# Ordering the loads of the state-space batches behind the load of the in-chunk kernel

## The chip, the cores and the metric

The kernel runs on one core of a Trainium2 chip. The metric is the device time of one launch in microseconds (us); before the change the median of three runs is 1145.79 us (1145.49 to 1152.16). A core has engines that each work through their own queue in order: PE (TensorE, matrix products), DVE (VectorE), ACT (ScalarE), POOL (GpSimd) and SP (SyncE, which here issues most of the transfers). An instruction whose inputs aren't there holds up all that stands behind it on its engine, and that goes for a transfer on SP's queue too.

## The reference, cut to what matters

The reference is a two-layer streaming encoder over 1024 frames of width 1024. Layer 0 has a state-space branch beside a retention branch, each multiplied by a SiLU gate; layer 1 is a convolution module. The change touches the state-space branch alone. For each of 64 groups of 16 channels it runs a diagonal complex recurrence with 64 states:

```
bu = einsum('tbgh,gnh->tbgn', u_c, bb)      # inputs into the states, bb complex
x  = scan: x[t] = a * x[t-1] + bu[t]        # a complex, diagonal
y  = einsum('tbgn,ghn->tbgh', x, c) + d * u_c   # real part
```

## The kernel before, in words

The kernel takes the frames in 128 blocks of 8. Inside a block the result is a product of u with an in-chunk kernel; between the blocks the states are carried by a scan. The 64 groups are worked off in eight batches of 8 groups, B = 0 to 7. The loop in `layer0_front` runs over sixteen gate blocks (nb = 8 to 23, two for each batch). A gate block has two halves of 24 matmuls (`mm_g`, each 128x512). Around them, in the order of the program text, stand for batch B:

- `s5_states(B)`: the load of u for the batch (tile `U`, L850); the matmuls `v` (L868), which put u through the two matrices `W2r` and `W2i`; on DVE the turning of `v`, the two scans over the blocks (L883) and the shifted states `S` (L890 to L896); the matmuls `kp` (L902, L903), which give the in-chunk kernel; its copies `Kg` (L905 on ACT, L906 on DVE), its transpose `kt` on PE (L908), its copy `Kt` on ACT (L910); the store of `Kt` to DRAM (L912); and the load of the same kernel in shifted form, tile `Wd` (L915), which ACT copies into `W1` (L917).
- the first gate block.
- `s5_out(B-1)`: the matmuls `y` of the batch before, u times `W1` (L932) and `S` times `W3` (L938), and their copies `yb`.
- the second gate block.
- `s5_tables(B+1)`: on POOL eighteen products for the tables of the next batch (`Mr`, `Mi`, `Tc`, `Ts`, `W3`); on ACT four copies that make `R8` (L839), the factors of the next scan; and for B+1 of 2 and more `s5_w2(B+1)`, which loads the spread tables `PTr`, `PTi`, `BTr` and `BTi` (L799 and L802, 256 KB each) and makes `W2r` and `W2i` out of them in six DVE instructions (L806 to L811). For batches 0 and 1 `W2` comes from transposes on PE instead.

Most of these tiles have one buffer: `PT`, `BT`, `W2`, `R8`, `S`, `W1`, `Mr`, `Mi`. `U` has two. `Wd` and the copies `yb` share a single buffer. The weights of the gate blocks come in by `wf_g` (L187 on SP), are rounded by ACT (`wh_g`, L189), and DVE forms the remainder (`wl_g`, L190). The gate results leave PSUM through DVE (`gt`, L393) and ACT (L394).

The order on each engine is fixed at build time by a list scheduler, which takes the ready instruction that stands first in the program text. `tc.issue_after(x)` adds a rule of order to it: what the block traces on the engine of x is put behind x in that engine's queue. It is an order of issue alone and waits for nothing to finish. Before the change one such rule exists here: the spread tables of batch B+1 are queued behind `self.u_load`, which at that point is the load of `U` for batch B.

Of the kernel before, what the change touches and what calls it, by code (L numbers as in the profile page):

```python
# [19 lines left out]
P = 128  # L20
# [50 lines left out]
class Trunk:  # L71
# [22 lines left out]
    def plan(self):  # L94

        A = self.A

        seq = [(A["w_u01"][nb] if nb < 2 else A["w_ab"][nb], f"u{nb}") for nb in range(8)]
        seq += [(A["w_ab"][nb], f"g{nb}") for nb in range(8, 24)]
        for p in range(4):  # L100
            seq += [(A["w_ab"][28 + p], f"k{p}"), (A["w_ab"][24 + p], f"q{p}")]

            if p == 0:
                seq += [(A["w_v"][j], f"v{p}_{h}_{j}") for h in range(2) for j in range(4)]
            elif p > 1:
                seq += [(A["w_v"][2 * p + i], f"v{p}_{i}") for i in range(2)]
        self.ws_d = self.dram.tile([2, 2, P, 2, KB, P], F32, name="ws_d")
        quad = lambda i, j, m: A["w_glu"][i, m, :, j]
        sums = lambda n, m: self.ws_d[n // 2, m, :, n % 2]
        glu = [q for m in range(2) for q in (quad(0, 0, m), quad(0, 1, m))]  # L110
        glu += [q(m) for q in (lambda m: sums(0, m), lambda m: sums(2, m), lambda m: quad(1, 1, m)) for m in range(2)]
        glu += [sums(n, m) for m in range(2) for n in (3, 1)]
        seq += [(q, f"glu{i}") for i, q in enumerate(glu)]

        def wo(h):
            return [q for nb in range(8) for q in ((A["w_out"][nb], f"wos{nb}_{h}"),
                                                   (A["w_out"][8 + nb], f"wor{nb}_{h}"))]

        def ab(h):
            return [q for nb in range(8) for q in ((A["w_c"][8 + nb], f"cb{nb}_{h}"),  # L120
                                                   (A["w_c"][nb], f"ca{nb}_{h}"))]
        def cg(h, nbs):
            return [(A["w_c"][16 + nb], f"cg{nb}_{h}") for nb in nbs]
        seq += wo(0) + wo(1)[:4] + ab(0) + wo(1)[4:] + cg(0, range(G0)) + ab(1) + cg(0, range(G0, 8))
        seq += cg(1, range(G0))
        seq += [(A["w_out_c"][nb], f"woc{nb}_{h}") for h in range(2) for nb in range(8)]
        self.wseq, self.wissued, self.wgot = seq, {}, 0
        self.low_load, self.early_low = {}, None
        self.wnames, self.lo_d = {n for _, n in seq}, {}

    def wnext(self, name, ahead=2):
# [659 lines left out]
    def s5_w2(self, B):  # L791

        nc, v = self.nc, self.nc.vector
        (ptr, pti), (btr, bti) = ([self.big(f"{n}{c}_{B}", f"{n}{c}", 1) for c in "ri"] for n in ("PT", "BT"))
        dp, db = self.pt_d, self.bt_d

        with self.tc.issue_after(self.u_load.ins):
            for c, (pt, bt) in enumerate(((ptr, btr), (pti, bti))):
                nc.sync.dma_start(pt[:].rearrange("p q n -> p (q n)"),  # L799
                                  bass.AP(tensor=dp.tensor, offset=dp.offset + (c * 2 * P + 4 * B) * P,  # L800
                                          ap=[[32 * P, 8], [0, 16], [1, 4 * P]]))
                nc.sync.dma_start(bt[:].rearrange("p q n -> p (q n)"),  # L802
                                  bass.AP(tensor=db.tensor, offset=db.offset + (c * 4 * P + 4 * B) * P,
                                          ap=[[0, 8], [32 * P, 16], [1, 4 * P]]))
        w2r, w2i = (self.big(f"W2{nm}_{B}", f"W2{nm}", 1) for nm in "ri")
        v.tensor_tensor(w2r[:], ptr[:], btr[:], op=ALU.mult)  # L806
        v.tensor_tensor(w2i[:], ptr[:], bti[:], op=ALU.mult)
        v.tensor_tensor(ptr[:], pti[:], bti[:], op=ALU.mult)
        v.tensor_tensor(pti[:], pti[:], btr[:], op=ALU.mult)
        v.tensor_tensor(w2r[:], w2r[:], ptr[:], op=ALU.subtract)  # L810
        v.tensor_tensor(w2i[:], w2i[:], pti[:], op=ALU.add)  # L811
        return [w2r, w2i]
# [29 lines left out]
    def s5_states(self, B):  # L842
        nc, w = self.nc, self.s5
        gp, v = nc.gpsimd, nc.vector
        q0 = 4 * B
        Mr, Mi, W3, Tc, Ts, R8, W2 = self.s5_tab.pop(B)


        U = w.tile([P, 8, P], F32, name=f"U_{B}", tag="U", bufs=2)
        self.u_load = nc.sync.dma_start(U[:], self.u_d[B].rearrange("j h g m -> (j h) g m"))  # L850


        first, W2 = W2 is None, W2 or []
        for nm, M in (("r", Mr), ("i", Mi)) if first else ():
            ps = self.bank(f"w2{nm}_{B}")
            for q in range(4):
                nc.tensor.transpose(ps[:, q * P:(q + 1) * P], M[:, q, :], self.ident[:])
            t = self.big(f"W2{nm}_{B}", f"W2{nm}", 1)
            nc.scalar.copy(t[:].rearrange("p q n -> p (q n)"), ps[:])
            W2.append(t)  # L860

        V = []
        for c in range(2):
            ps = self.bank(f"v{c}_{B}")
            for q in range(4):
                for g2 in range(2):
                    r = slice(64 * g2, 64 * g2 + 64)
                    nc.tensor.matmul(ps[r, q * P:(q + 1) * P], W2[c][:, q, r], U[:, 2 * q + g2, :],  # L868
                                     start=True, stop=True)
            V.append(ps)  # L870
        fl = lambda t: t[:].rearrange("p q n -> p (q n)")

        tc, ts = fl(Tc), fl(Ts)
        vr, vi = V[0][:], V[1][:]
        t2, t4 = (fl(self.big(f"m{i}_{B}", "tmpV", 4)) for i in range(2))
        v.tensor_tensor(t2, vi, ts, op=ALU.mult)
        v.tensor_tensor(t4, vr, ts, op=ALU.mult)
        v.tensor_tensor(vr, vr, tc, op=ALU.mult)
        v.tensor_tensor(vi, vi, tc, op=ALU.mult)
        v.tensor_tensor(vr, vr, t2, op=ALU.add)  # L880
        v.tensor_tensor(vi, vi, t4, op=ALU.subtract)
        for z in (vr, vi):
            v.tensor_tensor_scan(z, fl(R8), z, 0.0, op0=ALU.mult, op1=ALU.add)  # L883

        S = w.tile([P, 2, 4, P], F32, name=f"S_{B}", tag="S", bufs=1)
        c1 = lambda t: t[:, :, 1:P]
        c0 = lambda t: t[:, :, 0:P - 1]
        zr, zi = (z.rearrange("p (q n) -> p q n", q=4) for z in (vr, vi))
        t2, t3 = (self.big(f"d{i}_{B}", "tmpV", 4) for i in range(2))
        v.tensor_tensor(c0(t2), c0(zi), c0(Ts), op=ALU.mult)  # L890
        v.tensor_tensor(c0(t3), c0(zr), c0(Ts), op=ALU.mult)
        v.tensor_tensor(c0(zr), c0(zr), c0(Tc), op=ALU.mult)
        v.tensor_tensor(c0(zi), c0(zi), c0(Tc), op=ALU.mult)
        v.tensor_tensor(c1(S[:, 0]), c0(zr), c0(t2), op=ALU.subtract)
        v.tensor_tensor(c1(S[:, 1]), c0(zi), c0(t3), op=ALU.add)
        v.memset(S[:].rearrange("p c q m -> p (c q) m")[:, :, 0:1], 0.0)  # L896


        kp = self.bank(f"kp_{B}")
        for q in range(4):  # L900
            o = kp[q * 32:(q + 1) * 32, :P]
            nc.tensor.matmul(o, self.cbr[:, q0 + q, :], Mr[:, q, :], start=True, stop=False)  # L902
            nc.tensor.matmul(o, self.cbni[:, q0 + q, :], Mi[:, q, :], start=False, stop=True)  # L903
        Kg = w.tile([P, P], F32, name=f"Kg_{B}", tag="Kg", bufs=1)
        nc.scalar.copy(Kg[:, 16:], kp[:, 16:P])  # L905
        v.tensor_tensor(Kg[:, :16], kp[:, :16], self.dd[:, B, :], op=ALU.add)  # L906
        kp = self.bank(f"kt_{B}")
        nc.tensor.transpose(kp[:, :P], Kg[:], self.ident[:])  # L908
        Kt = w.tile([P, P], F32, name=f"Kt_{B}", tag="Kg", bufs=1)
        nc.scalar.copy(Kt[:], kp[:, :P])  # L910

        nc.sync.dma_start(self.k_d[B, 112:], Kt[:])  # L912
        Wd = w.tile([P, 8, P], F32, name=f"Wd_{B}", tag="yb", bufs=1)
        kd = self.k_d[B]
        nc.sync.dma_start(Wd[:], bass.AP(tensor=kd.tensor, offset=kd.offset, ap=[[P, P], [16 * P, 8], [1, P]]))  # L915
        W1 = w.tile([P, 8, P], F32, name=f"W1_{B}", tag="W1", bufs=1)
        nc.scalar.copy(W1[:].rearrange("p g (i h) -> p i g h", i=8), Wd[:].rearrange("p i (g h) -> p i g h", g=8))  # L917
        self.s5_back[B] = U, W1, W3, S
# [1009 lines left out]
```

## Time and profile before

| | |
|---|---|
| runs, median (lowest to highest) | 1145.79 us (1145.49 to 1152.16) |
| span of the profiled execution | 1149.0 us, 17198 instructions |
| device time of the profiled execution | not given apart from its span |
| PE busy | 1125.3 us, 98% of the span |
| PE weight load busy | 986.1 us, 86% |
| DVE busy | 847.4 us, 74% |
| ACT busy | 489.5 us, 43% |
| POOL busy | 654.3 us, 57% |
| mean granted TensorE clock | 0.991 |

In the rows "SPq" and "ACTq" are transfers as their queue issues them; their duration is the issue, not the transfer. Times are microseconds from the start of the span, and the number behind the time is the duration. A bracket at the end of a row holds the idle time ahead of it on its engine and what ended it. A row of a view by windows has the stretch, its length, then the busy time of PE, PE weight load, DVE, ACT and POOL with the number of instructions, then the granted clock, the share of the transfer engines in use and GB/s.

### The profile page before, as it was taken

What the parts mean: (1) busy time and instruction counts of PE and PEld (TensorE: products, weight loads), DVE (VectorE), ACT (ScalarE), POOL (GpSimd) and SP (SyncE); (2) the same over time, 40 slices, a digit from 0 to 9 for tenths busy, and PEclk for the clock granted to TensorE, in tenths of its full rate; (3) what the DMA queues carried; (4) which work ended last, traced back from release to release, by engine and by line L of the source; (5) the groups of instructions that cost most, each with busy time, mean ns of one, the idle gap of its engine ahead of it and who ended that gap; (6) DMA issues with size and microseconds to landing.
All of it is one profiled execution on the core that took longest, in us unless ns stands there. A gap on an engine that the chain in (4) does not pass through costs nothing.

```text
span 1149.0 us, 17198 instructions
## 1 busy us (share of the span) xinstructions
PE 1125.3 (98%) x6286; PEld 986.1 (86%) x6286; DVE 847.4 (74%) x1464; ACT 489.5 (43%) x719; POOL 654.3 (57%) x448
## 2 busy tenths in 40 slices
PE   9999999999999999989899999999999999999997
PEld 7888878888888889889788888888888888888787
DVE  6975788887418469484669622599999889999844
ACT  6423222333223231322446523555545677444674
POOL 2059999999246354232476011489544568677663
PEclk9999999999999999989899999999999999999999
DMA  9344445556388766858999988665778755357865
GB/s 352 111 134 154 122 164 177 179 174 206 114 279 290 241 220 186 292 171 304 348 382 308 342 287 282 185 240 202 239 256 293 242 188 175 119 182 257 287 226 193
DMA packets 117636, 261.45 MB, mean 228 GB/s; under 512 B 10672, under 2 KB 42288, under 8 KB 116912
## 3 DMA queue, kind: packets, MB, share of 16 engines
q1 hardware_dynamic: 114096, 247.78, 64.1%
q10 hardware_dynamic: 3456, 12.58, 2.9%
q8 instruction: 49, 0.80, 0.3%
q14 instruction: 35, 0.29, 0.1%
HBM read 181.48 MB, written 74.65 MB: 223 GB/s over the span
## 4 chain that ended last, share of the span: by engine, by line
PE 74%; DVE 13%; DMA 5%; issue 3%; POOL 3%; ACT 2%; SPq 0%; POOLq 0%; DVEq 0%; ACTq 0%
DVE cv L1535 5%; PE mm_wo L201 5%; PE mm_wo L200 5%; PE mm_wo L202 5%; PE mm_g L200 4%; PE mm_g L201 4%; PE mm_g L202 4%; PE mm_b L201 2%; PE mm_b L202 2%; PE mm_b L200 2%; PE mm_a L202 2%; PE mm_a L201 2%; PE mm_a L200 2%; PE mm_u L202 2%; PE mm_u L200 2%
## 5 line engine op out<-in xcount | busy, mean ns | idle before, releaser
L1535 DVE SCALAR_TENSOR_TENSOR cv<-u,convw,cv 128x512 f32<-128x512 f32 x398 | 273.0, 748 | 6.8 <-ACT cv L1514 4.8
L1508 POOL TENSOR_TENSOR tp<-tp,tp 128x512 f32<-128x512 f32 x64 | 82.9, 1296 | 33.9 <-ACT tp L1507 32.8
L200 PE MATMUL mm_g<-xh,wh_g 128*128 128x512 f32 x256 | 99.4, 388 | 0.0
L201 PE MATMUL mm_g<-xl,wh_g 128*128 128x512 f32 x256 | 98.1, 383 | 0.0
L202 PE MATMUL mm_g<-xh,wl_g 128*128 128x512 f32 x256 | 97.9, 382 | 0.0
L437 POOL TENSOR_TENSOR s1q<-s1q,s1q 128x512 f32<-128x512 f32 x12 | 17.1, 1427 | 81.4 <-ACT s1q L432 81.4
L1507 ACT ACTIVATE tp<-u,convw 128x512 f32<-128x512 f32 x64 | 45.4, 719 | 35.6 <-POOL tp L1508 34.8
L200 PEld LDWEIGHTS mm_g<-xh,wh_g 128*128 128x128 f32 x256 | 48.8, 191 | 8.7 <-issue 1.2
L202 PEld LDWEIGHTS mm_g<-xh,wl_g 128*128 128x128 f32 x256 | 48.8, 191 | 7.1
L201 PEld LDWEIGHTS mm_g<-xl,wh_g 128*128 128x128 f32 x256 | 48.7, 190 | 6.9 <-issue 0.4
L190 POOL TENSOR_TENSOR wl_v<-wf_v,wh_v 128x1024 fp32r<-128x1024 f32 x12 | 31.0, 2590 | 38.0 <-ACT wh_v L189 38.0
L190 POOL TENSOR_TENSOR wl_glu<-wf_glu,wh_glu 128x1024 fp32r<-128x1024 f32 x14 | 35.1, 2506 | 30.7 <-ACT wh_glu L189 30.7
L202 PE MATMUL mm_oc<-zh,wl_woc 128*128 128x512 f32 (+1 forms) x144 | 51.0, 357 | 0.3 <-DMA wl_woc<-lo_woc 0.3
L201 PE MATMUL mm_oc<-zl,wh_woc 128*128 128x512 f32 (+1 forms) x144 | 51.1, 356 | 0.0
L200 PE MATMUL mm_oc<-zh,wh_woc 128*128 128x512 f32 (+1 forms) x144 | 50.7, 363 | 0.0
L201 PE MATMUL mm_u<-xl,wh_u 128*128 128x512 f32 x128 | 48.5, 381 | 0.7 <-DVE xl L316 0.7
L200 PE MATMUL mm_wo<-ysh,wh_wos 128*128 128x512 f32 x128 | 48.9, 382 | 0.0
L200 PE MATMUL mm_g<-h1h,wh_cg 128*128 128x512 f32 x128 | 48.9, 382 | 0.0
L201 PE MATMUL mm_b<-h1l,wh_cb 128*128 128x512 f32 x128 | 48.7, 381 | 0.1
L202 PE MATMUL mm_b<-h1h,wl_cb 128*128 128x512 f32 x128 | 48.6, 380 | 0.0
L201 PE MATMUL mm_wo<-ysl,wh_wos 128*128 128x512 f32 x128 | 48.5, 379 | 0.0
L202 PE MATMUL mm_wo<-ysh,wl_wos 128*128 128x512 f32 x128 | 48.5, 379 | 0.0
(526 smaller groups left out, 3613.3 us busy)
## 6 DMA issues: line engine op xcount, KB each, us to landing
wf_g<-w_ab SPq DMA_DIRECT2D x16, 512.0 KB
wf_wos<-w_out SPq DMA_DIRECT2D x16, 512.0 KB
wf_wor<-w_out SPq DMA_DIRECT2D x16, 512.0 KB
wf_cb<-w_c SPq DMA_DIRECT2D x16, 512.0 KB
wf_ca<-w_c SPq DMA_DIRECT2D x16, 512.0 KB
wf_woc<-w_out_c SPq DMA_DIRECT2D x16, 512.0 KB
wf_v<-w_v SPq DMA_DIRECT2D x12, 512.0 KB
wf_cg<-w_c SPq DMA_DIRECT2D x11, 512.0 KB
```

The costliest lines, as they stand in the source:

```text
L190: self.low_made = lo[i].tensor_tensor(wl[:].rearrange(fl)[:, c], wf[:, c], h.bitcast(F32), op=ALU.subtract)
L200: nc.tensor.matmul(ps, wh[:, kb, :], xh, start=start, stop=False, **more)
L201: nc.tensor.matmul(ps, wh[:, kb, :], xl, start=False, stop=False, **more)
L202: self.last_mm = nc.tensor.matmul(ps, wl[:, kb, :], xh, start=False, stop=stop, **more)
L437: nc.gpsimd.tensor_tensor(a, a, sq[:], op=ALU.add)
L1507: nc.scalar.mul(sk[:], u[:, k:k + HALF], cw[:, nb, k:k + 1])
L1508: gp.tensor_tensor(s0[:], s0[:], sk[:], op=ALU.add)
L1535: v.scalar_tensor_tensor(dst[:], *tap, accs_[i][:], op0=ALU.mult, op1=ALU.add)
```

## The change

It stores the handle of the load of `Wd` and adds two rules of order on SP's queue. The load of `U` for a batch is queued behind the load of `Wd` that was traced last (batch B behind B-1; batch 0 has none). The loads of the spread tables are queued behind the load of `Wd` that was traced last as well as behind that of `U`. No transfer and no instruction is added or removed.

```
-        self.low_load, self.early_low = {}, None
+        self.low_load, self.early_low, self.wd_load = {}, None, None
...
         # s5_w2
-        with self.tc.issue_after(self.u_load.ins):
+        with self.tc.issue_after(self.u_load.ins), self.tc.issue_after(self.wd_load.ins):
             for c, (pt, bt) in enumerate(((ptr, btr), (pti, bti))):
                 nc.sync.dma_start(pt...)
                 nc.sync.dma_start(bt...)
...
         # s5_states
-        self.u_load = nc.sync.dma_start(U[:], self.u_d[B].rearrange("j h g m -> (j h) g m"))
+        with self.tc.issue_after(self.wd_load.ins) if self.wd_load else nullcontext():
+            self.u_load = nc.sync.dma_start(U[:], self.u_d[B].rearrange("j h g m -> (j h) g m"))
...
-        nc.sync.dma_start(Wd[:], bass.AP(tensor=kd.tensor, ...))
+        self.wd_load = nc.sync.dma_start(
+            Wd[:], bass.AP(tensor=kd.tensor, ...))
```

More of the change, by code (lines that the diff above doesn't have):

```diff
@@ L914, in s5_states @@
         kd = self.k_d[B]
-        nc.sync.dma_start(Wd[:], bass.AP(tensor=kd.tensor, offset=kd.offset, ap=[[P, P], [16 * P, 8], [1, P]]))
+        self.wd_load = nc.sync.dma_start(
+            Wd[:], bass.AP(tensor=kd.tensor, offset=kd.offset, ap=[[P, P], [16 * P, 8], [1, P]]))
         W1 = w.tile([P, 8, P], F32, name=f"W1_{B}", tag="W1", bufs=1)
```

## The prediction

> **What bounds the kernel now.** I read the head of the page first, then the waits of PE over the whole span, then busy time by windows in the state-space stage, which lies between about 83 and 322 us.
>
> ```profile
> span 1149.0 us, 17198 instructions
> ...
> PE 1125.3 (98%) x6286; PEld 986.1 (86%) x6286; DVE 847.4 (74%) x1464; ACT 489.5 (43%) x719; POOL 654.3 (57%) x448
> ```
>
> ```profile
> PE kt L908 <- DVE Kg L906: 2.0, 1, 2.0
> ```
>
> ```profile
> 180.00:208.00 28.00, 28.00 (x197) 24.34 (x195) 23.66 (x28) 8.21 (x15) 27.53 (x20) 1.00 0.54 179
> ```
>
> PE is busy in all 28.00 us of a typical batch at full clock, and the wait for `Kg` is the only one that the list of PE's waits has for this stage. So PE sets the time here, and a change of order can win no more than this one wait and what it drags along. But DVE (23.66) and POOL (27.53 of 28) have little room, so it can lose.
>
> **Where the transfers stand on SP now.** The next view is SP's queue in order of time, one early batch and one later.
>
> ```profile
> 139.31 0.38 SPq L850 DMA_DIRECT2D U<-u_d  x1
> 139.80 0.61 SPq L799 DMA_DIRECT2D PTr<-pt_d  x1
> 140.51 0.41 SPq L915 DMA_DIRECT2D Wd<-k_d  x1
> ...
> 169.13 0.38 SPq L915 DMA_DIRECT2D Wd<-k_d  x1
> 169.60 0.53 SPq L850 DMA_DIRECT2D U<-u_d  x1
> 170.22 0.60 SPq L799 DMA_DIRECT2D PTr<-pt_d  x1
> ...
> 196.93 0.38 SPq L915 DMA_DIRECT2D Wd<-k_d  x1
> ```
>
> The `Wd` at 140.51 is that of batch 1, and `U` of batch 2 and a table of batch 3 go ahead of it. From batch 2 on the order is already Wd(B), U(B+1). The tables that begin at 170.22 follow U(3): they are those of batch 4, and they stand ahead of Wd(3) at 196.93. The diff traces them behind `s5_states(3)`, so the new rule puts them behind that Wd(3). **The rule on U moves little; the rule on the tables moves them by most of a batch**, in six batches (2 to 7).
>
> **Part 1, what goes: the wait at 161 us.**
>
> ```profile
> 150.23 1.04 ACT L917 COPY W<-Wd 128x1024 f32<-128x1024 f32 x1 [9.48 <-DMA Wd<-k_d]
> ```
>
> ```profile
> 153.92 1.83 DVE L190 TENSOR_TENSOR wl_g<-wf_g,wh_g 128x1024 fp32r<-128x1024 f32 x1 [3.82 <-ACT wh_g L189]
> ```
>
> ```profile
> 161.21 0.33 PE L908 MATMUL kt<-ident,Kg 128*128 128x128 f32 x1 [2.03 <-DVE Kg L906]
> ```
>
> ```profile
> 162.00:163.00 1.00, 1.00 (x4) 0.83 (x4) 1.00 (x2) 0.00 (x0) 1.00 (x2) 0.60 0.00 0
> 163.00:164.00 1.00, 1.00 (x4) 0.72 (x4) 1.00 (x2) 0.00 (x0) 1.00 (x2) 0.50 0.00 0
> 164.00:165.00 1.00, 1.00 (x4) 0.81 (x3) 1.00 (x2) 0.00 (x0) 0.92 (x2) 0.50 0.00 0
> 165.00:166.00 1.00, 1.00 (x5) 0.81 (x4) 1.00 (x2) 0.00 (x0) 1.00 (x1) 0.69 0.00 0
> ```
>
> Read downward: ACT stands 9.48 us for Wd(1), which shares the transfer engines with U and the tables; behind it in ACT's queue is the rounding `wh_g`, for it DVE stands 3.82 us, so `Kg` comes late, and PE stands 2.03 us for it. Then the clock is granted at 0.60, 0.50, 0.50 and 0.69: 0.40 + 0.50 + 0.50 + 0.31 = 1.7 us of full speed lost. With Wd(1) ahead of U(2) and the tables this chain goes: **-3.7 us** (2.0 + 1.7). If the chain is only cut in part, nothing is won below 0.
>
> The price of a wait isn't always the same.
>
> ```profile
> 1078.31 1.13 PE L509 MATMUL cst<-cs,ones 128*128 128x512 f32 x2 [2.69 <-DVE cs L1617]
> ```
>
> ```profile
> 1078.00:1080.00 2.00, 1.62 (x3) 0.59 (x4) 2.00 (x4) 2.00 (x4) 0.72 (x1) 1.00 0.97 309
> ```
>
> This longer wait of 2.69 us left the clock at 1.00. The Trainium skill, "TensorE: Matmul & The Clock Gate", Part 1, says that the clock falls to half only after at least one idle window of about 3.4 us. By that rule the 2.03 us would have cost only themselves, and the sum below would be 1.7 us higher; the rows at 162 to 166 us speak against it, the row at 1078 us for it, so the measured case is used where it happened.
>
> **Part 2, what comes: W2 gets late.** The rows of PE for `v`, then batch 7 as a template, since it has no `W2` work of a following batch on DVE.
>
> ```profile
> 126.56 1.09 PE L868 MATMUL v<-U,W2r 128*64 128x128 f32 x16
> ...
> 149.30 1.09 PE L868 MATMUL v<-U,W2r 128*64 128x128 f32 x16
> ...
> 180.72 1.09 PE L868 MATMUL v<-U,W2r 128*64 128x128 f32 x16
> ...
> 208.21 1.09 PE L868 MATMUL v<-U,W2r 128*64 128x128 f32 x16
> 209.13 1.04 PE L868 MATMUL v<-U,W2i 128*64 128x128 f32 x16
> ```
>
> ```profile
> 290.67 1.09 PE L868 MATMUL v<-U,W2r 128*64 128x128 f32 x16
> ```
>
> ```profile
> 296.44 2.33 DVE L883 TENSOR_TENSOR_SCAN v<-R,v 128x512 f32<-128x512 f32 x2
> ```
>
> ```profile
> 193.66 1.28 ACT L839 ACTIVATE R<-s_s_m,s_r 128x128 f32<-128x128 f32 x4 [9.90 <-DVE v L883]
> ```
>
> ```profile
> 299.91 0.33 SPq L912 DMA_DIRECT2D k_d<-Kt  x1
> 301.49 0.38 SPq L915 DMA_DIRECT2D Wd<-k_d  x1
> ```
>
> Today Wd(3) is issued 16.2 us behind v(3) (196.93 - 180.72). One reason is that three `W2` instructions stand ahead of the scans on DVE, and ACT makes `R8` behind the scans and `Kt` only then. With late tables those three stand behind the scans. In batch 7 the scans end 8.1 us behind `v` (296.44 + 2.33 - 290.67); `R8` adds 1.28, the copy of `Kt` some 0.3, an estimate; and `Wd` follows the store of `Kt` by 1.58. So Wd(B) comes about 11.3 us behind v(B), an estimate: 192.0 for batch 3.
>
> ```profile
> 278.00:282.00 4.00, 4.00 (x43) 3.54 (x43) 4.00 (x6) 1.20 (x2) 3.92 (x4) 1.00 0.88 259
> 303.00:305.00 2.00, 2.00 (x17) 1.89 (x16) 0.69 (x1) 1.28 (x2) 0.15 (x1) 1.00 0.78 228
> ```
>
> The 512 KB of Wd(7), issued at 301.49, move in 303 to 305 us (2.00 us at 228 GB/s, 0.46 MB), so Wd(3) is in by 195.5. The four tables are issued directly behind it at 0.6 us each and hold 1 MB; at the 259 GB/s of the first row that is 4 us, the first pair by 197.5, the second by 199.5. No buffer holds them up, since the products of the batch before are long done.
>
> Now DVE in one batch:
>
> ```profile
> 180.50:208.10 27.60, 6.62 (x4) 1.00 0.54 176
> ```
>
> ```profile
> L190 DVE TENSOR_TENSOR wl_g<-wf_g,wh_g 128x1024 fp32r<-128x1024 f32 x2 | 3.2, 1597 | 0.2 <-ACT wh_g L189 0.2
> L393 DVE TENSOR_TENSOR gt<-mm_g,R 128x512 f32<-128x512 f32 x4 | 2.7, 679 | 3.7 <-PE mm_g L202 3.7
> ...
> L811 DVE TENSOR_TENSOR W2i<-W2i,PTi 128x512 f32<-128x512 f32 x1 | 1.5, 1525 | 0.0
> ...
> L809 DVE TENSOR_TENSOR PTi<-PTi,BTr 128x512 f32<-128x512 f32 x1 | 0.9, 869 | 0.0
> ...
> L895 DVE TENSOR_TENSOR S<-v,d 128x508 f32<-128x508 f32 x1 | 0.7, 670 | 0.0
> ```
>
> The first row is the four instructions on tile `PTr`. With L811 and L809 the six cost 6.62 + 1.53 + 0.87 = 9.0 us. Between 197.5 and `v` DVE also has one `wl_g` (1.6), two `S` (1.35) and at least one `gt` (0.7): 3.65. So `W2i` is ready at 197.5 + 9.0 + 3.65 = 210.2, and PE wants it at 209.13: **1.1 us late**, from 0 up (below 0 is excluded, PE being full today). If only PE's queue keeps its order, `v` holds up the gate matmuls behind it. Each of batches 3 to 7 pays it again, because Wd(B) hangs on v(B): 5 x 1.1 = **+5.5 us**, with the clock taken as unhurt by so short a wait.
>
> Batch 2 is tighter: v(1) to v(2) are only 22.7 us (149.30 - 126.56). By the same steps W2i(2) is ready at 126.56 + 11.3 + 5.5 + 12.65 = 156.0 against 150.2, so 5.8 us late and 1.7 us of clock, together 7.5, if the order of PE stays; nothing if gate matmuls go ahead of v(2). Two ends with no row between: I take the middle, **+3.7 us**.
>
> **Part 3, U.**
>
> ```profile
> 83.25 0.81 SPq L850 DMA_DIRECT2D U<-u_d  x2
> ...
> 114.89 0.37 SPq L915 DMA_DIRECT2D Wd<-k_d  x1
> ```
>
> U(0) and U(1) go out together at 83.25; now U(1) comes behind Wd(0), issued at 114.89, and v(1) is at 126.56. The 11 us between cover it against the 7.5 us that 1 MB took above (3.5 + 4), so it costs nothing; without that cover it would be the time by which U(1) lands behind 126.56. The later ones keep their place. `Wd` waits on SP for the store of `Kt` as today, and the same `wf_g` loads stand behind it.
>
> **The sum**: -3.7 + 5.5 + 3.7 = +5.5 us on the profiled span of 1149.0. That execution's own time isn't given, and its span lies 3.2 us above the median of the runs, so I add the difference to the median: 1145.8 + 5.5 = 1151 us.
>
> **The rivals.**
>
> Hidden: the scheduler sees `W2` late and puts gate matmuls, or `kp` and the whole chain to `Wd`, ahead of `v`. `kp` needs nothing of `v`, which speaks for it; that `kp` and `v` stand side by side in each batch today speaks against. Then only part 1 is left: 1145.8 - 3.7 = 1142 us.
>
> Slower: Wd(B) stays 16.2 us behind v(B), because the order on ACT or DVE isn't loosened. Then `W2i` is ready 4.9 us later than reckoned, 6.0 us late, and with 1.7 us of clock each of five batches pays 7.7: 38.5, with 7.5 for batch 2 and -3.7 that is +42, 1188 us. The point from which it decides is W2i behind 209.13, 28.4 us after v(3); halfway (3.5 us late, with clock 5.2 a batch) it gives 26 + 7.5 - 3.7 = +30, 1176 us. For it: DVE and POOL are nearly full, and `wl_g` and `gt` of higher rank can push `W2` back. Against it: the template of batch 7.
>
> Nothing: the queue's order stays. The row at 170.22 ahead of 196.93 all but excludes it: 1146 us.
>
> Faster by over 1%: 11.5 us would be half of the 24 us in which PE is idle at all (1149.0 - 1125.3), by new orders in later stages.
>
> **How the numbers follow.** Forecast 0.42 (1144 to 1157), hidden 0.28, nothing 0.02, slower 0.25 (1160 to 1188), faster 0.03. A range of 1141 to 1180 leaves out half of the worst slower case and the faster one. A measurement here can tell about 1% from no change, 11.5 us: forecast, hidden and nothing fall within it, 0.72; slower 0.25; faster 0.03.
>
> **What would show it.** Tables behind Wd(B) on SP; ACT's wait for Wd(1) under 4 us and no wait of PE for `Kg`; waits of PE for `W2r` or `W2i` of about 1 us in batches 3 to 7; v to v near 28.6 us instead of 27.5. The prediction is wrong if `Wd` comes neither near 11 us behind `v` nor `W2` takes about 12.7 us from its tables, or if PE's order changes.

## The result and the profile after

The changed kernel takes 1175.7 us (median of four runs, 1174.85 to 1177.17) against 1147.45 us for the kernel before among the same runs: a ratio of 1.024, 95% interval 1.021 to 1.028. It is slower by 2.4%. The head of the page of the changed kernel:

```profile
span 1175.4 us, 17176 instructions
...
PE 1130.7 (96%) x6286; PEld 992.1 (84%) x6286; DVE 832.4 (71%) x1464; ACT 489.0 (42%) x719; POOL 641.7 (55%) x448
```

The span is 26.4 us longer (1175.4 against 1149.0), while PE does the same 6286 matmuls in 5.4 us more of busy time. The other 21 us are idle time, and the waits of PE over the whole span say where:

```profile
PE v L869 <- DVE W2r L810: 24.0, 5, 6.7
...
PE v L869 <- issue: 1.1, 1, 1.1
```

Columns are the total in us, how many times, and the longest. PE now waits for `W2r` in front of `v`, 24.0 us in five waits, and no wait for `Kg` is left. Next, the state-space stage from 127 to 330 us as one window, of the kernel before and of the changed one (columns as in the table of before):

```profile
127.00:330.00 203.00, 200.97 (x1410) 175.20 (x1407) 150.86 (x188) 57.35 (x103) 164.76 (x116) 0.99 0.49 163
```

```profile
127.00:330.00 203.00, 177.87 (x1212) 154.79 (x1209) 130.91 (x181) 49.42 (x93) 146.69 (x113) 0.94 0.45 143
```

The granted clock falls from 0.99 to 0.94, and the same stretch holds 1212 matmul records instead of 1410. The timeline of PE places the loss batch by batch; these are the `v` of batches 1 to 4 and of batch 7:

```profile
125.97 1.09 PE L869 MATMUL v<-U,W2r 128*64 128x128 f32 x16
...
157.40 1.98 PE L869 MATMUL v<-U,W2r 128*64 128x128 f32 x16 [6.68 <-DVE W2r L810]
...
188.12 1.98 PE L869 MATMUL v<-U,W2r 128*64 128x128 f32 x16 [3.74 <-DVE W2r L810]
...
218.18 1.09 PE L869 MATMUL v<-U,W2r 128*64 128x128 f32 x16 [1.14 <-issue]
...
316.52 1.97 PE L869 MATMUL v<-U,W2r 128*64 128x128 f32 x16 [5.23 <-DVE W2r L810]
```

From v(1) to v(7) it takes 190.55 us, against 164.11 in the kernel before (126.56 to 290.67). The difference is 26.4 us, the whole difference of the spans. A batch takes 31.8 us on average (190.55 / 6) instead of 27.4. In one batch, batch 3, SP's queue and then DVE read so:

```profile
199.49 0.33 SPq L913 DMA_DIRECT2D k_d<-Kt  x1
201.06 0.38 SPq L916 DMA_DIRECT2D Wd<-k_d  x1
201.53 0.60 SPq L799 DMA_DIRECT2D PTr<-pt_d  x1
202.19 0.58 SPq L802 DMA_DIRECT2D BTr<-bt_d  x1
202.82 0.58 SPq L799 DMA_DIRECT2D PTi<-pt_d  x1
203.44 1.05 SPq L802 DMA_DIRECT2D BTi<-bt_d  x1
```

```profile
190.85 1.23 DVE L190 TENSOR_TENSOR wl_g<-wf_g,wh_g 128x1024 fp32r<-128x1024 f32 x1 [1.03 <-ACT wh_g L189]
191.99 0.68 DVE L877 TENSOR_TENSOR m<-v,Ts 128x512 f32<-128x512 f32 x1
...
195.67 2.33 DVE L884 TENSOR_TENSOR_SCAN v<-R,v 128x512 f32<-128x512 f32 x2
...
208.40 1.41 DVE L806 TENSOR_TENSOR W2r<-PTr,BTr 128x512 f32<-128x512 f32 x1 [2.40 <-DMA BTr<-bt_d]
214.59 1.43 DVE L807 TENSOR_TENSOR W2i<-PTr,BTi 128x512 f32<-128x512 f32 x1 [4.78 <-DMA BTi<-bt_d]
...
217.99 0.68 DVE L811 TENSOR_TENSOR W2i<-W2i,PTi 128x512 f32<-128x512 f32 x1
```

SP has the order that the rule asks for: the four tables of batch 4 go out directly behind Wd(3). But DVE stands 2.40 us for `BTr` and then 4.78 us for `BTi`; `BTi` lands 11.1 us after its issue (203.44 to 214.59). The chain of waits for 126 to 330 us has six such landings, one for each batch from 2 to 7; these are the first and the longest (start, duration):

```profile
141.19 11.17 DMA BTi<-bt_d
...
235.77 13.44 DMA BTi<-bt_d
```

This closes a loop for each batch: v(B), scans, `R8` and `Kt` on ACT, store of `Kt`, issue of Wd(B), landing of the tables of B+1, `W2`, v(B+1). PE's 27.5 us of work for a batch (208.21 to 235.70 in the kernel before, where it waits for nothing) fits into it with time to spare, so the loop sets the time.

### The profile page after: what moved, and what is told of

Same layout as the page of the kernel before. It is cut to its first block, busy times and chain, and to the rows that moved or that the text cites. A ratio compares the mean times of both kernels' runs of the same rounds, so it can differ in the third digit from the quotient of the medians.

```text
span 1175.4 us, 17176 instructions
## 1 busy us (share of the span) xinstructions
PE 1130.7 (96%) x6286; PEld 992.1 (84%) x6286; DVE 832.4 (71%) x1464; ACT 489.0 (42%) x719; POOL 641.7 (55%) x448
## 4 chain that ended last, share of the span: by engine, by line
PE 56%; DVE 22%; DMA 12%; issue 3%; ACT 3%; SPq 2%; POOL 1%; POOLq 0%; DVEq 0%; ACTq 0%
DVE cv L1537 11%; DMA BTi<-bt_d 6%; PE mm_wo L202 4%; PE mm_wo L200 4%; PE mm_wo L201 4%; PE mm_glu L200 2%; PE mm_glu L201 2%; PE mm_glu L202 2%; PE mm_u L202 2%; PE mm_u L200 2%; PE mm_u L201 2%; PE mm_oc L202 1%; PE mm_oc L201 1%; PE mm_oc L200 1%; PE mm_g L200 1%
## 5 line engine op out<-in xcount | busy, mean ns | idle before, releaser
L394 ACT ACTIVATE gt<-gt 128x512 f32<-128x512 f32 x32 | 20.1, 628 | 98.6 <-DVE gt L393 98.6
```

The source lines that it names most:

```text
L394: nc.scalar.activation(gt[:, c], gt[:, c], AF.Silu)
```

## The experiments

### Which of the two rules costs the time

Only the rule on `U`, the tables' rule left as it was:

```
-        with self.tc.issue_after(self.u_load.ins), self.tc.issue_after(self.wd_load.ins):
+        with self.tc.issue_after(self.u_load.ins):
```

> The rule on U alone; the tables stay behind U only, so behind Wd of the batch before. Theory (the loss comes from the spread tables, which now start behind Wd of their own preceding batch): the loss is gone and the wait of PE for Kg at 161 us too, 1142 to 1146 us, up to 0.4% under the kernel before. Rival (the rule on U carries a good part of the loss, by holding U until Wd is issued): over 1155 us, with PE waiting for v.

Measured: 1145.21 us (median of 12 runs, 1141.0 to 1148.9), ratio 0.998, interval 0.996 to 0.999. The first and last `v` and the window of the stage:

```profile
126.27 1.09 PE L869 MATMUL v<-U,W2r 128*64 128x128 f32 x16
...
286.44 1.09 PE L869 MATMUL v<-U,W2r 128*64 128x128 f32 x16
```

```profile
127.00:330.00 203.00, 203.00 (x1426) 177.54 (x1423) 154.69 (x189) 59.31 (x105) 168.38 (x117) 1.00 0.53 175
```

PE is busy in all 203.00 us at full clock. From v(1) to v(7) it takes 160.2 us in this execution, 3.9 less than before. The medians differ by less, 1.6 us (1146.81 to 1145.21; by the interval 0.7 to 4.7). So the rule on `U` costs nothing and wins Part 1, and this version is the fastest of the three: about 0.2% ahead of the kernel before.

Only the rule on the tables, without that on `U`:

```
-        with self.tc.issue_after(self.wd_load.ins) if self.wd_load else nullcontext():
-            self.u_load = nc.sync.dma_start(U[:], ...)
+        self.u_load = nc.sync.dma_start(U[:], ...)
```

> The rule on the tables alone; U is free. Theory (the tables carry the whole loss): 1172 to 1180 us, near the changed kernel's 1175.7. Rival (the loss needs both rules): under 1165 us.

Measured: 1178.65 us (1175.92 to 1180.88), ratio 1.026, interval 1.023 to 1.030. The whole loss is that of the tables' rule.

### An earlier issue

The tables are queued behind the store of `Kt` instead of behind `Wd`:

```
-        with self.tc.issue_after(self.u_load.ins), self.tc.issue_after(self.wd_load.ins):
+        with self.tc.issue_after(self.u_load.ins), self.tc.issue_after(self.kt_store.ins):
...
-        nc.sync.dma_start(self.k_d[B, 112:], Kt[:])
+        self.kt_store = nc.sync.dma_start(self.k_d[B, 112:], Kt[:])
```

> The changed kernel, but the tables are queued behind the store of Kt and not behind Wd, which waits about 1.5 us for that store to land. The last table is issued about 1.2 us earlier in each batch. Theory (a loop from v over Wd and the tables to the next v sets the length of a batch, so each microsecond comes six times): 6 x 1.2 = 7 us less, 1166 to 1171 us; v to v shorter by about 1.2 us. Rival (the tables land when the transfers of the stage allow, however early they start): 1174 to 1178 us, no change.

Measured: 1165.06 us (1163.0 to 1168.71), ratio 1.015, interval 1.012 to 1.017, which is 10.6 us below the changed kernel. SP's queue of batch 3, the landing of the same `BTi` from the chain of waits, and the last `v`:

```profile
198.71 0.33 SPq L913 DMA_DIRECT2D k_d<-Kt  x1
199.13 0.60 SPq L799 DMA_DIRECT2D PTr<-pt_d  x1
...
200.52 0.40 SPq L916 DMA_DIRECT2D Wd<-k_d  x1
...
201.65 1.17 SPq L802 DMA_DIRECT2D BTi<-bt_d  x1
```

```profile
201.65 10.01 DMA BTi<-bt_d
```

```profile
306.77 1.09 PE L869 MATMUL v<-U,W2r 128*64 128x128 f32 x16 [2.57 <-DVE W2r L810]
```

`BTi` goes out 2.94 us behind the store of `Kt` (201.65 - 198.71) instead of 3.95 (203.44 - 199.49). A batch takes 30.2 us ((306.77 - 125.82) / 6) instead of 31.8. The first pair gains more, since it now goes ahead of `Wd`: `PTr` goes out 0.42 us behind the store (199.13 - 198.71) instead of 2.04 (201.53 - 199.49). One rule changed, which moves the last issue by about a microsecond, shortens a batch by 1.6 us. That is what the loop says, and more than was expected of it; `BTi` also lands sooner (10.0 us here).

### What makes the landing slow

I tried three causes: rows that repeat (each table has 8 or 16 different rows, read into 128 partitions), the neighbours on the queue, and the form of the access. First the rows, all 128 different and contiguous (every table load reads the same 128 rows of `bt_d`, so the right tables are left out):

```
-    ap=[[0, 8], [32 * P, 16], [1, 4 * P]]        # and PT: [[32 * P, 8], [0, 16], [1, 4 * P]]
+    ap=[[4 * P, P], [1, 4 * P]]
```

> The changed kernel, with each table read from 128 different rows of 2 KB that lie one behind the other, where the kernel reads 8 or 16 rows over and over; the same bytes and the same 2 KB pieces. This leaves out the right tables. Theory A (the tables land 11 us after their issue because few rows are read many times): they land in about 5 us, the wait of PE for W2 nearly goes, 1146 to 1155 us. Theory B (they land late because U, weights and stores share the transfer engines): no change, 1172 to 1179 us.

Measured: 1156.6 us (1155.6 to 1164.54), ratio 1.009, interval 1.005 to 1.012. The landings from the view of line L802, `BTr` and `BTi` together, the timeline of PE, and for batch 3 the issue of `Wd` and the landing of `BTi`:

```profile
DMA to landing us min/median/max: 5.0/5.9/7.1
```

```profile
126.51 1.09 PE L869 MATMUL v<-U,W2r 128*64 128x128 f32 x16
...
153.20 1.09 PE L869 MATMUL v<-U,W2r 128*64 128x128 f32 x16 [1.94 <-issue]
...
182.00 1.41 PE L869 MATMUL v<-U,W2r 128*64 128x128 f32 x16 [2.59 <-issue]
...
211.38 1.09 PE L869 MATMUL v<-U,W2r 128*64 128x128 f32 x16
...
298.74 1.09 PE L869 MATMUL v<-U,W2r 128*64 128x128 f32 x16 [0.72 <-issue]
```

```profile
196.00 0.38 SPq L916 DMA_DIRECT2D Wd<-k_d  x1
```

```profile
197.99 7.00 DMA BTi<-bt_d
```

`BTr` and `BTi` land within 5.0 to 7.1 us, and a batch takes 28.7 us ((298.74 - 126.51) / 6). Two thirds of the loss are gone although the rule of order still stands. The neighbours next: the loads of `U` for batches 2 to 7 are left out, and `U` of batch 0 or 1 is used again:

```
+        if B < 2:
             U = w.tile(...)
             ... self.u_load = nc.sync.dma_start(U[:], ...)
+        else:
+            U = self.u_kept[B % 2]
```

> The changed kernel without the loads of U for batches 2 to 7, which use the u of batches 0 and 1 instead: 512 KB less right behind the tables on the same queue. Theory A (the tables read few rows many times and that makes them slow): the tables still land 10 us or more behind their issue, 1171 to 1177 us. Theory B (what follows on the queue slows them): the tables land about 2 us earlier, six times, 1160 to 1166 us.

Measured: 1174.9 us (1171.77 to 1177.07), ratio 1.024, interval 1.021 to 1.027: nothing won. The first and the last `BTi` in the chain of waits:

```profile
141.74 10.41 DMA BTi<-bt_d
...
298.97 12.14 DMA BTi<-bt_d
```

With half a megabyte less beside it, `BTi` lands hardly sooner: 10.4 to 12.1 us behind its issue, against 11.1 to 13.4. Then different rows again, but in the steps of the slow form, 8 by 16:

```
+    ap=[[4 * P, 8], [32 * P, 16], [1, 4 * P]]
```

> As the run with distinct rows (1156.6 us), but the 128 different rows are read in the kernel's own pattern for the B tables, in steps of 16 KB, 8 times over with an offset, so that no row is read twice within a load. This leaves out the right tables. Theory A1 (repeats of the same row are what is slow): stays near 1156 us. Theory A2 (steps of 16 KB are what is slow, whatever the repeats): goes back towards 1170 to 1176 us.

Measured: 1171.76 us (1169.71 to 1174.48), ratio 1.022, interval 1.019 to 1.025. The longest and the shortest landing of `BTi` in the chain of waits:

```profile
173.03 12.00 DMA BTi<-bt_d
...
204.71 9.50 DMA BTi<-bt_d
```

So the repeats are at most a small part of it, some 4 us of the whole time (1175.7 against 1171.76). What was left was either the 16 KB steps of the addresses or the first dimension of the pattern. The line of the page that counts the packets gives a first hint, for the run in 8 by 16 steps and for the run with contiguous rows:

```profile
DMA packets 117636, 261.45 MB, mean 223 GB/s; under 512 B 10672, under 2 KB 42288, under 8 KB 116912
```

```profile
DMA packets 117828, 261.45 MB, mean 226 GB/s; under 512 B 10864, under 2 KB 42480, under 8 KB 117104
```

The fast run has 192 packets more, all of them under 512 B, that is 8 for each of the 24 table loads. Two last runs, with the same 128 different rows:

```
+    ap=[[4 * P, 16], [64 * P, 8], [1, 4 * P]]     # 16 steps of 2 KB by 8 of 32 KB
```

> Each table load reads 128 different rows of the second table, as the two runs with different rows did, so W2 is not the reference's; its access pattern is written as 16 steps of 2 KB by 8 steps of 32 KB, where the slow run wrote 8 steps of 2 KB by 16 steps of 16 KB. The run with contiguous rows had 192 packets more than all others, all under 512 B: 8 for each of the 24 table loads. Theory A (the outer step of the pattern says over how many transfer engines a load is spread, 8 or 16): BTi lands 5 to 7 us behind its issue, 117828 packets, about 1157 us. Theory B (steps in the address are slow in HBM): BTi lands 9.5 to 12 us behind its issue, about 1172 us.

Measured: 1161.74 us (1159.64 to 1164.12), ratio 1.011, interval 1.007 to 1.015.

```profile
DMA to landing us min/median/max: 5.5/6.5/8.5
```

```profile
DMA packets 117828, 261.45 MB, mean 225 GB/s; under 512 B 10864, under 2 KB 42480, under 8 KB 117104
```

```
+    ap=[[64 * P, 8], [4 * P, 16], [1, 4 * P]]     # 8 steps of 32 KB by 16 of 2 KB: contiguous
```

> Each table load reads 128 contiguous rows, as in the run that was fast, so W2 is not the reference's; but the access pattern is written as 8 steps of 32 KB by 16 steps of 2 KB. Theory A (8 outer steps use 8 transfer engines): BTi lands 9.5 to 12 us behind its issue, 117636 packets, about 1172 us. Theory B (addresses in steps are slow, contiguous ones fast): BTi lands 5 to 7 us behind its issue, about 1157 us. If the two steps are merged into one before they reach the chip, the packets are 117828 and both theories expect 1157 us.

Measured: 1158.34 us (1155.66 to 1162.29), ratio 1.009, interval 1.006 to 1.012.

The first of the two decides it: the addresses jump by 32 KB, but with 16 outer steps instead of 8 the load has the 8 packets more and lands in 5.5 to 8.5 us. The second has the packets (117828, with 10864 under 512 B) and the time of the contiguous run, so the two steps were probably merged into one before they reached the chip; it tells nothing apart. **The number of steps in the outermost dimension makes the landing slow or fast, 8 or 16.** The trace shows no single transfer engine, but it has the share of them in use (last column but one; the last is GB/s). These are rows from the end of the tables and the loads queued behind them, in the changed kernel, in the run in 8 by 16 steps and in that in 16 by 8:

```profile
152.00:153.00 1.00, 0.00 (x0) 0.00 (x0) 0.62 (x1) 0.00 (x0) 0.97 (x1) 1.00 0.51 209
```

```profile
215.00:216.00 1.00, 1.00 (x5) 0.57 (x3) 1.00 (x1) 0.00 (x0) 0.91 (x1) 1.00 0.51 209
```

```profile
206.00:207.00 1.00, 1.00 (x7) 0.87 (x6) 1.00 (x1) 0.00 (x0) 1.00 (x2) 1.00 1.02 418
```

With 8 outer steps the rest of the work runs on half of the engines at half the rate; with 16 all are busy to the end. That 8 of the 16 carry such a load rests on this and on the 8 packets. A slowness of steps of 16 KB alone, which 32 KB would not have, was not tested by itself; it would not explain the half share or the packets. The Trainium skill, "DMA: Bandwidth & Descriptors", says under "Rules for kernel authors" that a leading dimension of c below 16, such as a zero-stride broadcast of c copies, confines the whole transfer to at most c engines, and under "Why a DMA increments its semaphore by 16 and not by 1" that each engine used posts one completion. Landings and packet counts here agree with both.

### Whether wait and clock add up

Fourteen spare matmuls, which nothing reads, stand ahead of `v` in batches 2 to 7, so that PE stays warm through its wait:

```
+            for _ in range(14 if B > 1 and c == 0 else 0):
+                nc.tensor.matmul(ps[:], self.ones_r[:], mv(self.xs[0][0][0][:]), start=True, stop=True)
```

> The changed kernel with 14 spare matmuls (128x512, 3.0 us at full clock) in front of v in batches 2 to 7, where PE otherwise waits for W2; their result is overwritten by v. Theory (each wait also costs about 1.7 us of clock behind it, some 10 us in all): PE's wait shrinks to under 3.4 us, the granted clock stays at or near 1.00 through the stage, and the time falls to 1163 to 1171 us although work is added. Rival (the wait alone counts, the clock is a side effect of the records): no gain, 1174 to 1182 us.

Measured: 1174.86 us (1171.32 to 1178.85), ratio 1.024, interval 1.020 to 1.029: no gain.

```profile
127.00:330.00 203.00, 194.02 (x1323) 169.11 (x1319) 129.90 (x182) 51.19 (x95) 148.91 (x114) 0.99 0.46 146
```

The clock is back at 0.99 (0.94 without the filling) and the time is the same, so warming PE through its wait wins nothing here. It doesn't show that a slow clock costs nothing. From v(3) at 189.46 us to v(5) at 250.48 PE waits for nothing in front of `v`, and a batch is 30.5 us, the 27.5 of before and some 3 us of spare work: there the filling itself sets the time. And `v` stands in the loop: in the changed kernel its half on `W2r` takes 1.98 us behind most waits instead of 1.09, in the rows above. How much of the loss is the clock's was not tested apart.

## Why the prediction was right and wrong

The range of 1141 to 1180 held the 1175.7 us, but only because it took in half of the slower rival: the sum itself, 1151, was 25 us too low. The prediction had "within 1%" as by far the likeliest; "slower" had 0.25.

**Part 1 was right.** PE no longer waits for `Kg`. ACT's wait for Wd(1) fell less than I wrote, to 5.34 us instead of under 4:

```profile
143.76 1.05 ACT L919 COPY W<-Wd 128x1024 f32<-128x1024 f32 x1 [5.34 <-DMA Wd<-k_d]
```

The run with the rule on `U` alone bounds the price: v(1) to v(7) shrinks by 3.9 us in the profiled executions, where 2.0 + 1.7 = 3.7 was forecast, and the medians by 1.6, within 0.7 to 4.7. In the profiles the clock's share counted, where PE was the bound of the stage; by the rule of the Trainium skill that the prediction weighed ("TensorE: Matmul & The Clock Gate", Part 1) it would have been 2.0, which the medians don't exclude.

**Part 2 had the right mechanism and a term of the wrong size: the landing of the tables.** I took 1 MB at 259 GB/s, 4 us, so that the second pair would be in 7.5 us behind the issue of `Wd`. In batch 3 `BTi` came 13.5 us behind it (214.59 - 201.06): 6.0 us more. The 259 GB/s was the rate at which all traffic ran in a window; a rate of the whole says nothing of what one load with 8 outer steps gets. The form of the loads, with 8 outer steps, stood in the kernel and was not used, nor was the landing of such a load in the chain of waits of the kernel before:

```profile
146.15 8.46 DMA PTi<-pt_d
```

Two more terms were off, in opposite directions. `Wd` was to come 11.3 us behind `v` and came 12.9 behind in batch 3 (201.06 - 188.12). The template, batch 7, has no PE wait; here `wl_g` stood ahead of `m` on DVE, so that `m` began 3.9 us behind `v` and the scans ended 9.9 us behind it instead of 8.1. And the work on `W2` got cheaper: `W2i` was to be ready 10.65 us after the second pair (11.3 + 5.5 + 12.65 - 18.8), but the five instructions behind the landing of `BTi` are through in 4.1 us (214.59 to 217.99 + 0.68). The first product had been made before, and the last, L811, took 0.68 us instead of the 1.53 of before. A window of the changed kernel over this work:

```profile
216.00:218.00 2.00, 1.04 (x5) 0.57 (x3) 1.93 (x5) 0.00 (x0) 0.00 (x0) 1.00 0.04 16
```

POOL, the last of the five busy times, does nothing there. In the run with contiguous rows, where the tables land sooner, POOL is still at work, and the same five instructions take 7.7 us (205.01 to 211.07 + 1.59):

```profile
205.00:213.00 8.00, 7.67 (x50) 6.37 (x51) 7.92 (x6) 0.00 (x0) 7.04 (x5) 1.00 0.37 153
```

```profile
211.07 1.59 DVE L811 TENSOR_TENSOR W2i<-W2i,PTi 128x512 f32<-128x512 f32 x1
```

So in these two traces the products take longer beside a busy POOL, and late tables make `W2` cheaper. That POOL is the cause was not tested by itself.

For batch 3 the three are +1.6 + 6.0 - 6.6 = 1.0 us, and its length of 30.1 us (188.12 to 218.18) is not far from the forecast 28.6. But batch 3 is the shortest. Over batches 2 to 6, on average, `Wd` comes 14.1 us behind `v` (forecast 11.3), `BTi` lands 14.7 us behind `Wd` (7.5), and the next `v` starts 3.0 us behind that (9.8, what is left of 28.6): +2.8 + 7.2 - 6.8 = +3.2, and a batch of 31.8 us. Summed over the stage: v(1) to v(2) got 8.7 us longer (31.43 against 22.74), where I took 3.7 out of a span of 0 to 7.5; v(2) to v(7) takes 159.1 us, 21.4 more than the five batches of 27.5 without a `Kg` wait (137.7), where I had 5.5. With -3.7 that is +26.4.

The run with contiguous rows shows what is left when this term is near its forecast: `BTr` and `BTi` land in 5.0 to 7.1 us, where the prediction has 5.1 for `BTi` (in 7.5 us behind `Wd`, issued 2.4 behind it as in batch 3). There v(1) to v(2) is 26.69 us, 3.95 longer than before (forecast 3.7), a batch from v(2) to v(7) 29.1 us (forecast 28.6), and the profiled span 1155.1, 6.1 above before (forecast 5.5). The rules of order are the same there, so the mis-sized landing carries about 20 of the 26 us. That the remainder meets the forecast so closely is in part luck: in batch 3 of that run `Wd` comes 14.0 us behind `v` (11.3), `BTi` lands 9.0 behind `Wd` (7.5), and `v` starts 6.4 behind that (9.8), so that two errors up and one down nearly cancel.

**Part 3 was right:** the rule on `U` costs nothing.

**The rivals.** The measured time is that of the slower rival's halfway point, 1176, but not for its reason. It had `Wd` up to 16.2 us behind `v`, held by ACT and DVE; the changed kernel has 12.9 us in batch 3 and up to 15.2 in batch 4 (233.39 - 218.18), so that this reason holds in part:

```profile
233.39 0.38 SPq L916 DMA_DIRECT2D Wd<-k_d  x1
```

The run with contiguous rows, under the same rules of order, shows the tables' landing to be the larger part. It also added 1.7 us of clock to each wait; the filled run, with the clock back at 0.99, won none of that back, though its spare work costs time of its own. The rival "hidden" did not occur: PE kept its order, with `v` waiting in front of the gate matmuls. The rival "nothing" is excluded by SP's queue.

## What to carry to other kernels

A rule of order from a late load to an early one can close a loop over the batches: add up the loop (work, issue, landing, work) and compare it with the bound engine's time for one batch, before asking what each move costs. Size the landing of a transfer by the same transfer in the trace, or by one with the same access pattern, not by bytes over the rate of a busy window, and look at the first dimension of the pattern. A wait and the slow clock behind it need not add up where a loop sets the time: keeping PE warm won nothing here.

## What the runs showed of the hardware

The same 256 KB of 128 rows land in 5.0 to 7.1 us when contiguous, in 5.5 to 8.5 us with 16 outer steps and 32 KB jumps, and in 9.5 to 12.0 us with 8 outer steps; the slow form has 8 packets fewer for each load, and at its end the share of the transfer engines in use is 0.51 at 209 GB/s, against 1.02 at 418. Repeated rows and the neighbours on the queue make little difference: 1175.7 us with repeats against 1171.8 without, and 1174.9 without the loads of `U`. The product `W2i` (L811, 128x512) takes 0.68 us on DVE while POOL is idle and 1.59 while it is busy 7.04 of 8 us.
